# Operand tiles in a pool of their own, other holds of the shared PSUM bank, deferred squares and split key-value products in a one-layer hybrid trunk

## The chip, the cores and the metric

The kernel runs on one core of one Trainium2 chip. The metric is the device time of one execution in microseconds; the time before is 2718.81 us, the median of 3 runs (2717.66 to 2721.08). All times below are in microseconds (us) unless marked ns.

## What is computed

One layer of a hybrid encoder trunk on an input of 2048 positions by 1024 channels, in float32. Cut to what matters:

```
xn   = rmsnorm(h)
proj = xn @ w_in                       # columns split among three mixers
att  = chunked softmax attention       # 6 heads of 64, own chunk of 64 and 8 before it
conv = GLU, causal depthwise conv of 31 taps, LayerNorm, swish, pointwise projection
ret  = retention in chunks             # 6 heads of 64, rotary q and k, state carried along
h    = h + concat(att, conv, ret) @ w_o
h    = h + square(relu(rmsnorm(h) @ w1)) @ w2            # hidden size 4096
h    = h + sigmoid(rmsnorm(h) @ w_pg) * (p @ w_ple)
```

The retention's state needs, per head and chunk, the product of the decayed keys with the values (64 by 64).

## The kernel before

**Blocks and stages.** The sequence is worked in four blocks of T = 512 positions (four tiles of 128). A block goes through these stages, each a generator that issues matmuls and yields after each: conv_proj; the gate of the block before, in two halves; att_proj and ret_proj in turn for three pairs of heads (ap and rp); wo_a and wo_b (the output projection); ffn1 and ffn2 in eight groups, with ffn1 one group ahead; the gate of the last block comes at the end. Every large product is in split precision: an operand is a high part in fp32r and a low part, and `mm3s` (line 173) issues three matmuls of 512 columns, high with high, high with low, low with high. The output projection has 48 + 16 products of this kind per block, a group of ffn2 has 32, and the gate has 64 with the normalised residual and 16 with p.

**Tiles in SBUF.** There is a pool for constants, and then one pool, sp, for all else. A tag of a pool gets its place at its first use. In the compiled kernel, in bytes of a partition: constants from 1,152; w, the split weights, six buffers of 8,192 from 23,584; big slot 0 at 72,736 and slot 1 at 89,120 (16,384 each); the kv buffers (keys, queries, values, residual h) from 105,696; the work tiles behind them, with the convolution's yh and yl in 150,752 to 161,631 and the gate's p operand (ph, pl) in 172,640 to 180,831; big slot 2 at 195,712 and slot 3 at 212,096, up to 228,479. Slots 0 and 1 hold xh and xl, the high and low part of the normalised input, for conv_proj, the projections, ffn1, and the gate of the last block (`x3` in ffn2, line 739). Slots 2 and 3 hold in turn the mixers' output (mh, ml, line 458), the hidden layer (hid, two groups in turn, line 713) and xh, xl of the gate of the other blocks (`late`, line 753). In ap and rp the weights are the moving operand; everywhere else the weights are stationary and the tile of a big slot moves.

**The chains.** The mixers' own steps are three chains, generators that yield a delay after each step: att_mix (chain 0), ret_mix (chain 1), conv_mix (chain 2). `advance` (line 883), called after each yield of a stage, issues a chain's next step when the planner's clock `clk` (a sum of matmul costs in us, lines 46 to 59) has passed the step's delay. Chains 1 and 2 share one PSUM bank, `rbank` (line 112, one buffer), so they also wait for `rfree`, which is set 2.0 us ahead after each of their steps. When the position reaches a chain's end (lines 871 to 878), its steps are issued without either wait:

```
if t[1] > pos and clk[0] < (t[4] if c is chains[0] else max(t[4], rfree[0])):
    break
...
d = next(t[3])
t[4] = clk[0] + d + 0.01
if c is not chains[0]:
    rfree[0] = clk[0] + 2.0
```

The order of TensorE's instructions is kept as issued, so TensorE stands still when a step finds the bank not yet read out or its operand not yet made. The delays are in `W` (line 261): r0 3.5 after rkv, the key-value products; r1 2.4 after the transposes rqT and rkT; r2 1.8 after each score product rsc; c1 5.0 after cvt, the transposes before the convolution's LayerNorm, whose z is made on VectorE with a step on GpSimd (lines 395 to 403); c2 4.0 after cvb and cpw; qk 5.0, st 4.5 and ts 2.0 in attention.

**Squares.** `rms_split` (line 230) makes, for each of 8 channel tiles of h, the high part on ScalarE (L233), the low part on VectorE (L234), the square on ScalarE and, from the second tile on, the sum of squares on VectorE (L240). It is called in wo_b, in late and in the last ffn2. The sums go through a matmul with ones (ms) and come back as the row scale.

**Priorities.** All other orders are those of the scheduler, which goes by program order; `tc.high_priority(offset=n)` puts instructions n places forward, a negative n back (LATE is -1000).

Of the kernel before, what the change touches and what calls it, by code (L numbers as in the profile page):

```python
# [17 lines left out]
P = 128  # L18
D = 1024
S = 2048  # L20
T = 512
# [11 lines left out]
HALF = 512  # L33
AHEAD = 2500
LATE = -1000
AT, RT = (2, 4, 6), (3, 5, 7)
WOA = [(j, k) for ks in ((0, 1, 2, 3), (4, 5)) for j in range(2) for k in ks] + [(j, k) for j in range(2, KT) for k in range(6)]

# [2 lines left out]
def trunk(ctx, tc, a, out):  # L41
# [4 lines left out]
    class PE:  # L46
# [10 lines left out]
        def transpose(o, x, i):  # L57
            clk[0] += 240 / 2200.0
            tc.keep_in_program_order(nc.tensor.transpose(o, x, i))  # L59

    cpool = ctx.enter_context(tc.tile_pool(name="const", bufs=1))
    sp = ctx.enter_context(tc.tile_pool(name="sp", bufs=1))
    dram = ctx.enter_context(tc.tile_pool(name="dram", bufs=1, space=bass.MemoryType.DRAM))
# [9 lines left out]
    def stile(tag, bufs, shape, name=None, dt=F32):  # L73
        return sp.tile(list(shape), dt, tag=tag, name=name or tag, bufs=bufs)
# [2 lines left out]
        return stile("raw", 2, [P, UNIT], name)  # L77

    def big(name, slot):
        return stile(f"big{slot}", 1, [P, 8, T], name, F32R)  # L80

    def anat(name):
        return stile("anat", 5, [P, 256], name)
# [36 lines left out]


    def wtile():
        return stile("w", 6, [P, 2, 2, HALF], "w", F32R)

    def wsplit(w, x, n, eng):
        A.activation(w[:, 0, :n], x, AF.Copy)  # L126
# [103 lines left out]
    def rms_split(j, gidx, x, sq):  # L230
        h = cur["h"][j]
        g = ng[:, gidx, j : j + 1]
        A.activation(x[0][:, j], h, AF.Copy, scale=g)  # L233
        V.scalar_tensor_tensor(x[1][:, j], h, g, f(x[0][:, j]), ALU.mult, ALU.subtract)  # L234
        if j == 0:
            A.activation(sq, h, AF.Square)
        else:
            q = tmp("q", T)
            A.activation(q, h, AF.Square)
            V.tensor_tensor(sq, sq, q, ALU.add)  # L240

    def rms_rstd(r):
        b = rbank("ms")
# [139 lines left out]
    def conv_mix():  # L383
# [3 lines left out]
        for u in range(2):  # L387
            b = rbank("cvt")
            b2 = b.rearrange("p (t n) -> p t n", n=DC)
            s6 = stile("s6", 2, [P, 20])  # L390
            for i in range(2):
                t = 2 * u + i
                for c in range(2):
                    PE.transpose(b2[:, i, c * P : c * P + P], ys[c][:, t * P : t * P + P], ident)
            for i in range(2):
                V.bn_stats(s6[:, 6 * i : 6 * i + 6], b2[:, i])
                V.bn_aggr(s6[:, 12 + 2 * i : 14 + 2 * i], s6[:, 6 * i : 6 * i + 6])
            mv = s6[:, 12:16].rearrange("p (t c) -> p t c", c=2)
            V.tensor_scalar(s6[:, 16:18], mv[:, :, 1], EPS, None, ALU.add)
            rstd(s6[:, 18:20], s6[:, 16:18], 2)  # L400
            for i in range(2):
                V.tensor_scalar(z[u][:, i * DC : i * DC + DC], b2[:, i], s6[:, 12 + 2 * i : 13 + 2 * i],
                                s6[:, 18 + i : 19 + i], ALU.subtract, ALU.mult)
            yield W["c1"]
        hl = []
        for c in range(2):
            b = rbank("cvb")
            for t in range(NT):
                PE.transpose(b[:, t * P : t * P + P], z[t // 2][:, (t % 2) * DC + c * P : (t % 2) * DC + c * P + P], ident)
            u = tmp("u", T)  # L410
            A.activation(ys[c], b, AF.Tanh, bias=cvh[:, 1, c : c + 1], scale=cvh[:, 0, c : c + 1])
            A.activation(u, b, AF.Identity, bias=cvh[:, 1, c : c + 1], scale=cvh[:, 0, c : c + 1])
            V.scalar_tensor_tensor(ys[c], ys[c], 1.0, u, ALU.add, ALU.mult)
            yh, yl = cv("yh", F32R), cv("yl", F32R)
            A.activation(yh, ys[c], AF.Copy)
            V.tensor_tensor(yl, ys[c], f(yh), ALU.subtract)
            hl.append((yh, yl))
            yield W["c2"]
        yield W["c3"]
        for c in range(2):  # L420
            b = rbank("cpw")
# [178 lines left out]
    def ret_mix(p):  # L600
# [5 lines left out]
        st[p].reverse()  # L606
        b = rbank("rkv")
        for t in range(NT):
            PE.matmul(b[:, t * P : t * P + P], ns[t][:, P : 2 * P], ns[t][:, 256:384], start=True, stop=True)
        states = [now] + stm + [nxt]  # L610
        for t in range(NT):
            for hr in hrs:
                V.scalar_tensor_tensor(states[t + 1][hr, hr], states[t][hr, hr], gstate[hr, p : p + 1],
                                       b[hr, t * P + hr.start : t * P + hr.stop], ALU.mult, ALU.add)
        yield W["r0"]
        b = rbank("rqT")
        for t in range(NT):
            PE.transpose(b[:, t * P : t * P + P], ns[t][:, :P], ident)
# [1 line left out]
        for h, hr in enumerate(hrs):  # L620
            V.tensor_copy(qz[hr, :, h], b[hr].rearrange("p (t n) -> p t n", n=P))
        A.activation(qT, b, AF.Copy)
        yield W["r1"]
        b = rbank("rkT")
        for t in range(NT):
            PE.transpose(b[:, t * P : t * P + P], ns[t][:, P : 2 * P], ident)
        kT = stile("ro", 1, [P, T], "rk")
        A.activation(kT, b, AF.Copy)
        yield W["r1"]
        at = stile("rat", 1, [P, NT, 2 * P])  # L630
        mask = rm.rearrange("p h n -> p (h n)").unsqueeze(1).to_broadcast([P, 2, 2 * P])
        for u in range(2):
# [219 lines left out]

    chains = [[], [], []]
    rfree = [0.0]

    def chain(i, gen, start, end):
        chains[i].append([start, end, gen, None, 0.0])
# [24 lines left out]

    def advance(pos):
        posn[0] = pos
        for t in list(tasks):
            while t[0] and t[0][0] <= pos:
                t[0].pop(0)
                if t[2] is None:
                    t[2] = t[1]()
                next(t[2], None)  # L890
            if not t[0]:
                for _ in t[2]:
                    pass
                tasks.remove(t)
        for c in chains:
            while c and c[0][0] <= pos:
# [4 lines left out]
                    t[3] = t[2]()  # L901
                try:
                    d = next(t[3])
                    t[4] = clk[0] + d + 0.01
                    if c is not chains[0]:
                        rfree[0] = clk[0] + 2.0
                except StopIteration:
                    c.pop(0)

# [146 lines left out]
```

## Time and profile before

| | |
|---|---|
| median of 3 runs | 2718.81 us |
| lowest and highest | 2717.66 and 2721.08 us |
| profiled execution, device time | 2718.58 us |
| its span in the trace | 2716.6 us |
| TensorE busy | 2680.4 us, 99% |
| VectorE busy | 1327.8 us, 49% |
| ScalarE busy | 764.2 us, 28% |
| GpSimd busy | 97.0 us, 4% |
| DMA, share of 16 engines | 55.7%, mean 196 GB/s |

The profiled execution takes 2.0 us more than its span, what lies ahead of the first and behind the last instruction. Matmuls are pipelined: a group's mean is from the start to the end of one, and a new one starts before the last has ended, so the pace of a stream is read from the start of a run of matmuls to the start of the next.

### The profile page before, as it was taken

What the parts mean: (1) busy time and instruction counts of PE and PEld (TensorE: products, weight loads), DVE (VectorE), ACT (ScalarE), POOL (GpSimd) and SP (SyncE); (2) the same over time, 40 slices, a digit from 0 to 9 for tenths busy, and PEclk for the clock granted to TensorE, in tenths of its full rate; (3) what the DMA queues carried; (4) which work ended last, traced back from release to release, by engine and by line L of the source; (5) the groups of instructions that cost most, each with busy time, mean ns of one, the idle gap of its engine ahead of it and who ended that gap; (6) DMA issues with size and microseconds to landing.
All of it is one profiled execution on the core that took longest, in us unless ns stands there. A gap on an engine that the chain in (4) does not pass through costs nothing.

```text
span 2716.6 us, 33597 instructions
## 1 busy us (share of the span) xinstructions
PE 2680.4 (99%) x13354; PEld 2216.5 (82%) x13354; DVE 1327.8 (49%) x2649; ACT 764.2 (28%) x1576; POOL 97.0 (4%) x98
## 2 busy tenths in 40 slices
PE   8989999999999999999999999999999999999999
PEld 7777788888888888888888888888888888888887
DVE  7966544458655443334755552222384545222233
ACT  4444423343244222123214331101222432110111
POOL 1010000000010000000001000000000100000000
PEclk9999999999999999999999999999999999999999
DMA  8667656467633567677543455555654354555553
GB/s 285 211 213 244 219 177 208 166 198 267 217 121 140 206 216 261 216 255 261 217 168 121 159 203 192 193 186 191 240 194 170 112 199 142 189 191 187 192 201 125
DMA packets 123708, 533.36 MB, mean 196 GB/s; under 512 B 12832, under 2 KB 39712, under 8 KB 77728
## 3 DMA queue, kind: packets, MB, share of 16 engines
q1 hardware_dynamic: 123552, 531.21, 55.7%
q8 instruction: 106, 1.74, 0.3%
q14 instruction: 50, 0.41, 0.0%
HBM read 410.58 MB, written 120.59 MB: 196 GB/s over the span
## 4 chain that ended last, share of the span: by engine, by line
PE 89%; DVE 6%; DMA 2%; POOL 1%; ACT 1%; issue 1%; SPq 0%; POOLq 0%; DVEq 0%; ACTq 0%
PE acc L54 52%; PE w L54 27%; PE ple L54 2%; PE po L54 2%; PE sc L54 2%; PE sc L59 1%; POOL ass L199 1%; PE rout L54 1%; DVE y L359 1%; PE cvp L54 1%; DMA w<-k_wr 1%; DVE w L127 1%; PE rsc L54 1%; POOL g L199 0%; PE cpw L54 0%
## 5 line engine op out<-in xcount | busy, mean ns | idle before, releaser
L54 PE MATMUL acc<-xh,w 128*128 128x512 f32 (+1 forms) x1744 | 546.7, 389 | 0.0
L54 PE MATMUL acc<-w,xh 128*128 128x512 f32 (+1 forms) x1536 | 457.5, 373 | 1.1 <-DMA w<-k_wr 1.1
L54 PEld LDWEIGHTS acc<-xh,w 128*128 128x128 f32 x1744 | 326.3, 188 | 70.5 <-ACT xh L233 0.2
L54 PE MATMUL acc<-hid,w 128*128 128x512 f32 x1536 | 373.7, 396 | 0.0
L54 PE MATMUL w<-hid,w 128*128 128x512 f32 x1536 | 368.8, 395 | 0.0
L54 PEld LDWEIGHTS w<-hid,w 128*128 128x128 f32 x1536 | 288.5, 188 | 69.9
L54 PEld LDWEIGHTS acc<-hid,w 128*128 128x128 f32 x1536 | 288.7, 188 | 69.7
L54 PE MATMUL acc<-xl,w 128*128 128x512 f32 (+1 forms) x872 | 337.4, 391 | 1.9 <-DVE xl L234 1.9
L54 PE MATMUL w<-xh,w 128*128 128x512 f32 x1024 | 323.3, 391 | 0.0
L54 PEld LDWEIGHTS acc<-w,xh 128*128 128x128 f32 x1536 | 280.8, 189 | 38.9 <-issue 6.3
L126 ACT ACTIVATE w<-raw 128x512 fp32r<-128x512 f32 (+1 forms) x288 | 163.4, 615 | 460.6 <-PE acc L54 190.3
L54 PE MATMUL acc<-w,xl 128*128 128x384 f32 (+1 forms) x768 | 284.2, 370 | 0.0
L721 ACT ACTIVATE hid<-r 128x512 fp32r<-128x512 f32 x128 | 80.0, 625 | 569.3 <-DVE r L720 569.3
L54 PEld LDWEIGHTS w<-xh,w 128*128 128x128 f32 x1024 | 192.8, 189 | 39.7
L54 PE MATMUL w<-xl,w 128*128 128x512 f32 x512 | 200.1, 391 | 0.0
L54 PEld LDWEIGHTS acc<-xl,w 128*128 128x128 f32 x872 | 163.9, 188 | 38.3 <-DVE xl L234 4.2
L127 DVE TENSOR_TENSOR w<-raw,w 128x512 fp32r<-128x512 f32 (+1 forms) x288 | 182.7, 676 | 23.8 <-ACT w L126 23.1
L747 DVE TENSOR_TENSOR h<-h,w 128x512 f32<-128x512 f32 x128 | 88.0, 687 | 205.7 <-PE w L54 205.3
L359 DVE SCALAR_TENSOR_TENSOR y<-gl,cw,y 128x512 f32<-128x512 f32 x240 | 172.5, 745 | 1.9
L747 DVE TENSOR_TENSOR h<-h,acc 128x512 f32<-128x512 f32 x128 | 87.9, 687 | 169.9 <-PE acc L54 169.5
L54 PEld LDWEIGHTS acc<-w,xl 128*128 128x128 f32 x768 | 145.5, 189 | 15.7 <-issue 0.5
L720 DVE SCALAR_TENSOR_TENSOR r<-acc,r 128x512 f32<-128x512 f32 x64 | 44.3, 691 | 210.6 <-PE acc L54 197.7
(177 smaller groups left out, 2811.9 us busy)
## 6 DMA issues: line engine op xcount, KB each, us to landing
w<-k_w SPq DMA_DIRECT2D x160, 1024.0 KB, 4.8
k_w<-w SPq DMA_DIRECT2D x64, 1024.0 KB, 7.1
raw<-in_w_dram SPq DMA_DIRECT2D x96, 512.0 KB, 4.4
w<-k_wr SPq DMA_DIRECT2D x36, 1024.0 KB, 7.1
w<-k_w_g SPq DMA_DIRECT2D x30, 1024.0 KB, 4.8
w<-k_wa SPq DMA_DIRECT2D x36, 768.0 KB, 5.6
w<-k_w_oa SPq DMA_DIRECT2D x18, 1024.0 KB, 7.0
k_wr<-w SPq DMA_DIRECT2D x12, 1024.0 KB, 7.3
```

What stands on the lines that cost most here:

```text
L54: tc.keep_in_program_order(nc.tensor.matmul(o, x, y, start=start, stop=stop))
L59: tc.keep_in_program_order(nc.tensor.transpose(o, x, i))
L126: A.activation(w[:, 0, :n], x, AF.Copy)
L127: eng.tensor_tensor(w[:, 1, :n], x, f(w[:, 0, :n]), ALU.subtract)
L199: G.tensor_tensor(o, var, nhalf[:, :n], ALU.pow)
L359: V.scalar_tensor_tensor(y, gl[:, j : j + T], cw[:, c, j : j + 1], y, ALU.mult, ALU.add)
L720: V.scalar_tensor_tensor(r, b, 0.0, cur["r2"], ALU.max, ALU.mult)
L721: A.activation(hid[:, j], r, AF.Square)
L747: V.tensor_tensor(h[j], h[j], b, ALU.add)
```

## The change

There are four edits. The tags of the big slots and of w move out of sp into a pool gp that is opened before the constants. The squares of rms_split and their sum are put 150 places back. The planner's yields may give a second number, the time for which the shared bank is held (2.0 where none is given); cvt holds it for 5.0, cvb for 3.0, rkv for 3.5, rqT and rkT for 2.4; and both delays and holds are multiplied by 1.2 up to the start of the output projection of block 0. The key-value product of a tile, 128 by 128 with only the two diagonal blocks of 64 by 64 in use, is issued as the two diagonal blocks alone.

```diff
--- before.py
+++ after.py
@@ -33,6 +33,7 @@
 HALF = 512
 AHEAD = 2500
 LATE = -1000
+SQ = -150
 AT, RT = (2, 4, 6), (3, 5, 7)
 WOA = [(j, k) for ks in ((0, 1, 2, 3), (4, 5)) for j in range(2) for k in ks] + [(j, k) for j in range(2, KT) for k in range(6)]
 
@@ -58,6 +59,7 @@
             clk[0] += 240 / 2200.0
             tc.keep_in_program_order(nc.tensor.transpose(o, x, i))
 
+    gp = ctx.enter_context(tc.tile_pool(name="gp", bufs=1))
     cpool = ctx.enter_context(tc.tile_pool(name="const", bufs=1))
     sp = ctx.enter_context(tc.tile_pool(name="sp", bufs=1))
     dram = ctx.enter_context(tc.tile_pool(name="dram", bufs=1, space=bass.MemoryType.DRAM))
@@ -77,7 +79,7 @@
         return stile("raw", 2, [P, UNIT], name)
 
     def big(name, slot):
-        return stile(f"big{slot}", 1, [P, 8, T], name, F32R)
+        return gp.tile([P, 8, T], F32R, tag=f"big{slot}", name=name, bufs=1)
 
     def anat(name):
         return stile("anat", 5, [P, 256], name)
@@ -120,7 +122,7 @@
 
 
     def wtile():
-        return stile("w", 6, [P, 2, 2, HALF], "w", F32R)
+        return gp.tile([P, 2, 2, HALF], F32R, tag="w", name="w", bufs=6)
 
     def wsplit(w, x, n, eng):
         A.activation(w[:, 0, :n], x, AF.Copy)
@@ -232,12 +234,13 @@
         g = ng[:, gidx, j : j + 1]
         A.activation(x[0][:, j], h, AF.Copy, scale=g)
         V.scalar_tensor_tensor(x[1][:, j], h, g, f(x[0][:, j]), ALU.mult, ALU.subtract)
-        if j == 0:
-            A.activation(sq, h, AF.Square)
-        else:
-            q = tmp("q", T)
-            A.activation(q, h, AF.Square)
-            V.tensor_tensor(sq, sq, q, ALU.add)
+        with tc.high_priority(offset=SQ):
+            if j == 0:
+                A.activation(sq, h, AF.Square)
+            else:
+                q = tmp("q", T)
+                A.activation(q, h, AF.Square)
+                V.tensor_tensor(sq, sq, q, ALU.add)
 
     def rms_rstd(r):
         b = rbank("ms")
@@ -401,7 +404,7 @@
             for i in range(2):
                 V.tensor_scalar(z[u][:, i * DC : i * DC + DC], b2[:, i], s6[:, 12 + 2 * i : 13 + 2 * i],
                                 s6[:, 18 + i : 19 + i], ALU.subtract, ALU.mult)
-            yield W["c1"]
+            yield W["c1"], 5.0
         hl = []
         for c in range(2):
             b = rbank("cvb")
@@ -415,7 +418,7 @@
             A.activation(yh, ys[c], AF.Copy)
             V.tensor_tensor(yl, ys[c], f(yh), ALU.subtract)
             hl.append((yh, yl))
-            yield W["c2"]
+            yield W["c2"], 3.0
         yield W["c3"]
         for c in range(2):
             b = rbank("cpw")
@@ -606,13 +609,15 @@
         st[p].reverse()
         b = rbank("rkv")
         for t in range(NT):
-            PE.matmul(b[:, t * P : t * P + P], ns[t][:, P : 2 * P], ns[t][:, 256:384], start=True, stop=True)
+            for h, hr in enumerate(hrs):
+                PE.matmul(b[hr, t * P + h * HD : t * P + h * HD + HD], ns[t][:, P + h * HD : P + h * HD + HD],
+                          ns[t][:, 256 + h * HD : 256 + h * HD + HD], start=True, stop=True)
         states = [now] + stm + [nxt]
         for t in range(NT):
             for hr in hrs:
                 V.scalar_tensor_tensor(states[t + 1][hr, hr], states[t][hr, hr], gstate[hr, p : p + 1],
                                        b[hr, t * P + hr.start : t * P + hr.stop], ALU.mult, ALU.add)
-        yield W["r0"]
+        yield W["r0"], 3.5
         b = rbank("rqT")
         for t in range(NT):
             PE.transpose(b[:, t * P : t * P + P], ns[t][:, :P], ident)
@@ -620,13 +625,13 @@
         for h, hr in enumerate(hrs):
             V.tensor_copy(qz[hr, :, h], b[hr].rearrange("p (t n) -> p t n", n=P))
         A.activation(qT, b, AF.Copy)
-        yield W["r1"]
+        yield W["r1"], 2.4
         b = rbank("rkT")
         for t in range(NT):
             PE.transpose(b[:, t * P : t * P + P], ns[t][:, P : 2 * P], ident)
         kT = stile("ro", 1, [P, T], "rk")
         A.activation(kT, b, AF.Copy)
-        yield W["r1"]
+        yield W["r1"], 2.4
         at = stile("rat", 1, [P, NT, 2 * P])
         mask = rm.rearrange("p h n -> p (h n)").unsqueeze(1).to_broadcast([P, 2, 2 * P])
         for u in range(2):
@@ -852,6 +857,7 @@
 
     chains = [[], [], []]
     rfree = [0.0]
+    slow = [1.0]
 
     def chain(i, gen, start, end):
         chains[i].append([start, end, gen, None, 0.0])
@@ -882,6 +888,7 @@
 
     def advance(pos):
         posn[0] = pos
+        slow[0] = 1.2 if pos < at(("woa", 0), 0.0) else 1.0
         for t in list(tasks):
             while t[0] and t[0][0] <= pos:
                 t[0].pop(0)
@@ -901,9 +908,10 @@
                     t[3] = t[2]()
                 try:
                     d = next(t[3])
-                    t[4] = clk[0] + d + 0.01
+                    d, r = d if isinstance(d, tuple) else (d, 2.0)
+                    t[4] = clk[0] + d * slow[0] + 0.01
                     if c is not chains[0]:
-                        rfree[0] = clk[0] + 2.0
+                        rfree[0] = clk[0] + r * slow[0]
                 except StopIteration:
                     c.pop(0)
```

## Rows read from the trace of the kernel before

**Rows 1.** The page: the span, and busy time, share and instructions of TensorE.

```profile
span 2716.6 us, 33597 instructions
PE 2680.4 (99%) x13354; PEld 2216.5 (82%) x13354; DVE 1327.8 (49%) x2649; ACT 764.2 (28%) x1576; POOL 97.0 (4%) x98
```

**Rows 2.** Waits of TensorE: who, for whom, us in total, times, longest.

```profile
PE cvb L59 <- DVE z L402: 4.0, 3, 1.3
PE rsc L54 <- DVE rat L638: 3.6, 5, 1.1
PE rkv L54 <- DVE z L402: 3.0, 1, 3.0
PE sc L54 <- DVE pT L516: 2.4, 2, 2.2
PE rkT L59 <- ACT rq L622: 2.1, 2, 1.3
PE acc L54 <- DVE xl L234: 1.9, 3, 0.8
PE cvb L59 <- ACT rq L622: 1.9, 1, 1.9
PE sc L54 <- ACT k L202: 1.8, 1, 1.8
PE sc L54 <- DVE k L203: 1.5, 2, 1.0
```

**Rows 3.** Stretches of block 0: length, busy us by engine; third from last, granted clock.

```profile
69.00:76.00 7.00, 6.54 (x19) 5.20 (x20) 6.65 (x17) 1.27 (x6) 0.00 (x0) 0.51 0.74 268
158.00:161.30 3.30, 3.12 (x17) 2.72 (x17) 0.97 (x5) 0.00 (x0) 0.00 (x0) 0.50 0.06 25
171.60:175.00 3.40, 3.40 (x20) 2.63 (x19) 1.41 (x3) 2.32 (x4) 0.00 (x0) 0.51 0.00 0
284.20:287.60 3.40, 3.40 (x9) 2.65 (x8) 1.51 (x3) 1.15 (x2) 0.00 (x0) 0.50 0.09 28
```

**Rows 4.** Chain that ended last, feed-forward of block 0: start, us, what.

```profile
353.33 10.88 PE w L54 x48
...
372.46 5.60 PE w L54 x24
```

**Rows 5.** Groups of matmuls, shapes apart, whole span: count, busy us, mean ns, idle.

```profile
L54 PE MATMUL acc<-hid,w 128*128 128x512 f32 x1536 | 373.7, 396 | 0.0
L54 PE MATMUL w<-hid,w 128*128 128x512 f32 x1536 | 368.8, 395 | 0.0
L54 PE MATMUL w<-xh,w 128*128 128x512 f32 x1024 | 323.3, 391 | 0.0
...
L54 PE MATMUL ple<-pl,w 128*128 128x512 f32 x62 | 24.5, 395 | 0.0
...
L54 PE MATMUL cpw<-yh,pww 128*128 128x512 f32 x32 | 11.6, 405 | 0.0
```

**Rows 6.** Same view: output projection of block 1, gates of blocks 2 and 3.

```profile
926.17 17.73 PE acc L54 x76
...
2020.12 5.60 PE acc L54 x24
...
2677.82 5.49 PE acc L54 x24
```

**Rows 7.** Waits of TensorE in the mixers' stages of block 1 alone.

```profile
PE rsc L54 <- DVE rat L638: 0.5, 1, 0.5
```

**Rows 8.** VectorE in order of time at the start of block 0's feed-forward.

```profile
280.55 0.74 DVE L234 SCALAR_TENSOR_TENSOR xl<-h,ng,xh 128x512 fp32r<-128x512 f32 x1
281.21 0.68 DVE L240 TENSOR_TENSOR sq<-sq,q 128x512 f32<-128x512 f32 x1
```

**Rows 9.** Chain that ended last, mixers of block 1.

```profile
768.64 0.89 PE rkv L54 x8
...
772.48 1.24 PE po L54 x20
```

## The prediction

> **What bounds the kernel now.** I read the head of the page first. TensorE is busy for 2680.4 us of 2716.6 [rows 1], so only what TensorE does, or waits for, counts. VectorE, ScalarE and the queues matter where TensorE stands still for them. Three things can then be gained: waits of TensorE, stretches at the lower clock, and a shorter step from one matmul to the next.
>
> The list of waits, limited to TensorE, is short [rows 2]. The rows shown add up to 22.2 us. All but one belong to the chains (attention, retention, convolution), whose steps are strewn among the projections. The exception waits for the low parts of the normalised residual at the start of the feed-forward stage (L234). The 3.0 us before rkv are one wait on z (L402): the retention chain asked for the shared bank while the convolution chain's statistics still read it.
>
> The table by stretches shows what such waits cost on top [rows 3]. In four stretches of block 0, 17.1 us together, the granted clock is 0.50 or 0.51, the 1.2 GHz level; the timeline puts waits of [rows 2] right before each: rkv's 3.0 us before 158, cvb's 1.9 on rq before 171.6, the scores' 1.8 and then 1.0 on k before 69, the three on xl, 1.9 in all, before 284.2. At half the clock, half of a busy stretch is lost: 3.5, 1.6, 1.7 and 1.7 us.
>
> The chain of work that ended last gives the step of the large matmuls. In the first feed-forward product 48 matmuls take 10.88 us, 226.7 ns each; in the second, 24 take 5.60 us, 233.3 ns each [rows 4]. Both have 512 moving columns and three matmuls per product. The averages over the whole trace say the same, 391 ns against 395 and 396 [rows 5]. What differs is the moving operand: slots 0 and 1 (bytes 72,736 to 105,503) in the first, hid in slots 2 and 3 (195,712 to 228,479) in the second. The gate is the better test, being the same code twice: for blocks 0 to 2 it reads slots 2 and 3, and 24 matmuls take 5.60 us; for block 3 it reads slots 0 and 1, and 24 take 5.49 us [rows 6]. The output projection, which reads slots 2 and 3, is at 17.73/76 = 233.3 ns. So the rate goes with the place of the moving operand.
>
> **The change part by part,** against the profiled execution: 2718.58 us, of which 2.0 lie around the span; it stands 0.2 under the median of 2718.81, so I take both as one.
>
> **A, the pool.** The new pool comes first, so w fills bytes 1,152 to 50,303 and slots 0 to 3 fill 50,304 to 115,839 (six times 8,192, four times 16,384). No moving operand of a projection lies high any more. hid: 2 x 1536 matmuls [rows 5] x 6.6 ns = 20.3 us. Output projection: 4 blocks x 64 products x 3 = 768 matmuls x 6.6 = 5.1. Gate of three blocks: 24 groups x 0.11 = 2.6 [rows 6]. Together 28.0. What lay between slots 1 and 2 moves up by 32,768 bytes. The gate's p operand lay high before and already takes 395 ns [rows 5], so it loses nothing. The keys under the scores (504 matmuls, two at a time) move from 105,696 to 138,464 and on; no row shows them there, so they cost between nothing and 252 x 6.6 ns = 1.7 us, and I take 1.0, above the middle, since every high operand in the rows is slow. Net -27.0. The bounds are -28 and -15: slot 3 ends in 99,456 to 115,839, and nothing in the rows reads beyond 105,503 fast, so half of the gain could stay away. Here a rule speaks against the change.
>
> The Trainium skill, "TensorE: Matmul & The Clock Gate", section "Back-to-back issue gap", gives a warm matmul of 512 columns 216 ns wherever its operand lies, and "SBUF — State Buffer", section "Who interferes with whom", says that TensorE never waits on anyone there; by these A would be 0 and the sum 2700. The trace has 226.7 and 233.3 ns and disagrees; the rows decide.
>
> **B, the chains.** In block 0 every own delay becomes 1.2 times as long, and a step that leaves long work behind keeps the bank reserved for longer (planner microseconds, which I take as real ones). rkv after cvt: 2.0 becomes 6.0, so the wait of 3.0 and its slow clock of 1.6 go: -4.6. cvb after rqT: 2.0 becomes 2.9: -0.9 of 1.9, and half of the 1.7, since the wait stays half as long. First scores, 1.8 + 1.0 behind k: the delay grows by 1.0, so -1.0; their 3.5 us of clock I count at -1.0, between 0 and -3.5, because nearly two thirds of the wait stay. Scores behind pT, 2.2: -0.9. rkT, two waits of 2.1 together, delay +0.5: -1.0. rsc, two of about 1.1, delay +0.4: -0.7. Together -11.0. In blocks 1 to 3 only the holds change. rsc loses 0.5 each [rows 7] because cvt slips in ahead of it; a hold of 5.0 instead of 2.0 sends rsc later: -1.5. The 1.3 us before cvb stay, for c1 was 5.0 already and z is late behind retention's VectorE work. B is -12.5. The bounds are -20 and +3: no row shows these chains with longer holds, and a later step can meet another wait. Behind a step held back waits only the rest of its own chain; the projections go on meanwhile. A chain that gets so late that it reaches its deadline issues without any delay; that is in the upper bound.
>
> **C, squares.** VectorE alternates xl (0.74 us) and sq (0.68) one for one [rows 8], while TensorE wants an xl per matmul. With the squares behind, xl comes every 0.6 us or so rather than every 1.26, and block 0 loses its 1.9 us and the slow clock, 1.7: -3.5. Blocks 1 to 3 have no such row and gain nothing. What could be late next is the mean-square matmul that reads sq; VectorE's work before it is the same in sum, so it is done by about the same moment, but TensorE gets there some 3.5 us earlier. Bounds -4 to +1.
>
> **D, key-value products.** Eight instructions in 0.89 us become sixteen with half the stationary and half the moving columns. The nearest row is po: 64 stationary columns, two halves side by side, 20 in 1.24 us, 62 ns each [rows 9], but 128 moving columns. Sixteen at 62 are 0.99, and 0.50 if half the columns halve it: per product +0.10 to -0.39, over 12 products +1.2 to -4.7. I take -2.0, near the middle.
>
> Sum: -27.0 - 12.5 - 3.5 - 2.0 = -45.0, so 2718.6 - 44.7 = **2674 us**. With every term at its good end it is 2662 (-28 -20 -4 -4.7), with every term at its bad end 2709 (-15 +3 +1 +1.2), for which four things have to go wrong at once.
>
> **The rivals.**
> 1. The place of the operand is not the cause, A is 0. For it: nothing in the page names a port or an address. Against it: the gate at two rates with the same code [rows 6]. Time: 2718.6 - 18.0 = 2700. (The two pages above would have it so.) Chance 0.10.
> 2. The longer holds give nothing: the waits in block 0 move to other steps, since VectorE has the same work to do, and the clock falls as before. For it: most of these waits are on VectorE, which the holds don't relieve [rows 2]. Against it: the longest, rkv's, is an order of steps that the holds forbid. Time: 2718.6 - 27.0 - 3.5 - 2.0 = 2686. Chance 0.18.
> 3. Slower: it is the start of the operand, not its height, that sets the rate. xh starts 32 bytes past a multiple of 64 (72,736) and is fast; hid starts on a multiple of 128 (195,712) and is slow. The new pool starts at 1,152, nine times 128, and all its tiles would be slow. Then A is no gain, and conv, first feed-forward product and last gate, 384 + 3072 + 192 matmuls, pay 6.6 ns (24 us), and the projections that move w pay 1152 x 6.6 + 1152 x 5.0 (13 us): 2718.6 + 37 - 18.0 = 2738. It decides once some 2,700 of these matmuls slow down (18.0 / 6.6 ns). Against it: pl and yh (172,640 and on, and 150,752 and on, all 32 past a multiple of 64) take 395 and 405 ns, not the 391 of xh [rows 5]. Chance 0.04.
> 4. The parts cancel within the noise. Chance 0.03.
>
> **How the numbers follow.** The forecast has what is left, 0.65. Two runs of this kernel differ by up to 0.13%, so 0.2%, or 5.4 us, is what a measurement can tell from no change. Faster: 0.65 + 0.18 + 0.10 = 0.93; same 0.03; slower 0.04. The range takes in the forecast with its bounds and rival 2, and half of rival 1: 2660 to 2700.
>
> **What would show it.** A: the chain has 24 matmuls of the second feed-forward product in about 5.45 us instead of 5.60, and 5.49 in the gate of every block. If hid still takes 396 ns on average, A is wrong; if xh rises to 396, it is rival 3. B: no wait of rkv on z, and a granted clock of 1.00 in the stretch that answers to 158; sc behind k still waits. If the waits of TensorE in block 0 add up to over 15 us, rival 2. C: no wait on L234, and no new one before ms. D: a rkv group under 0.89 us. Wrong altogether it would be if the span stayed over 2705.

## The result, and the profile after

The changed kernel takes 2681.54 us, the median of 4 runs (2681.03 to 2685.79), beside 2718.23 us for the kernel before (4 runs, 2716.89 to 2721.08): a ratio of 0.9867, with a 95% interval of 0.9850 to 0.9884. By the ratio that is 36.2 us less (gains of runs below are also given by their ratio, taken on 2718 us). It lies within the range given, 7.5 us over the forecast of 2674. The profiled execution took 2681.23 us. Two single executions, 8963.00 us of e1_pool below (its profiled one) and 5370.15 us of the kernel before, are left out of all figures. The head of its page answers to [rows 1]: the span is 37.2 us shorter, and TensorE is busy for 34.3 us less.

```profile
span 2679.4 us, 33782 instructions
PE 2646.1 (99%) x13450; PEld 2209.8 (82%) x13450; DVE 1328.7 (50%) x2649; ACT 765.3 (29%) x1576; POOL 96.5 (4%) x98
```

**The pace of the matmuls.** The chain that ended last, of the changed kernel (start, us, what), answers to [rows 4], [rows 6] and [rows 9]:

```profile
344.47 10.88 PE w L55 x48
...
363.51 5.44 PE w L55 x24
...
754.52 0.62 PE rkv L55 x16
...
915.79 12.52 PE acc L55 x55
...
1990.05 5.46 PE acc L55 x24
1995.51 1.40 PE ple L55 x6
```

The first feed-forward product keeps its 226.7 ns (10.88/48). The second has come down to the same pace: 24 matmuls in 5.44 us instead of 5.60. The gate of block 2 takes 5.46 instead of 5.60, and the output projection 227.6 ns a matmul (12.52/55) instead of 233.3. A key-value group (rkv) takes 0.62 us instead of 0.89. Only the matmuls of the gate's p operand (ple) are at 233.3 ns (1.40/6); in the kernel before they were a little faster, at 230 (1.38/6, shown with the table below). The groups by form, which answer to [rows 5], say the same (count, busy us, mean ns):

```profile
L55 PE MATMUL acc<-hid,w 128*128 128x512 f32 x1536 | 363.1, 389 | 0.0
L55 PE MATMUL w<-hid,w 128*128 128x512 f32 x1536 | 358.6, 389 | 0.0
L55 PE MATMUL w<-xh,w 128*128 128x512 f32 x1024 | 323.1, 391 | 0.0
...
L55 PE MATMUL ple<-pl,w 128*128 128x512 f32 x62 | 24.6, 396 | 0.0
```

**The waits.** TensorE's waits in the changed kernel (who, for whom, us, times, longest) answer to [rows 2]:

```profile
PE cvt L60 <- DVE z L405: 5.8, 3, 1.9
PE cvt L60 <- DVE y L362: 3.6, 1, 3.6
PE sc L55 <- DVE pT L519: 2.3, 2, 2.0
PE ms L55 <- DVE sq L243: 1.9, 2, 1.7
PE cpw L55 <- DVE ml L431: 1.6, 1, 1.6
...
PE sc L55 <- DVE k L205: 1.0, 1, 1.0
PE sc L55 <- ACT k L204: 0.9, 1, 0.9
PE rkT L60 <- ACT rq L627: 0.9, 2, 0.5
...
PE cvb L60 <- DVE z L405: 0.7, 1, 0.7
```

The rkv wait of 3.0 us is gone, as are those of rsc (3.6), of cvb on rq (1.9) and of the residual's low part (1.9). In their place stand four that the kernel before did not have: cvt on z, cvt on y, ms on sq, cpw on ml. With the lines left out, and without the opening waits of cvp, the list adds up to 21.0 us; the same list of before adds up to 23.8 ([rows 2] and 1.6 us in two small lines). So 2.8 us of waiting went away, while the names on it changed almost wholly.

**The clock.** Four stretches of 3.4 us are at the 1.2 GHz level (length, busy us by engine, granted clock third from last); the fifth line is the stretch that answers to the one after rkv's wait in [rows 3], now at the full clock:

```profile
92.60:96.00 3.40, 3.40 (x14) 2.87 (x15) 2.27 (x7) 1.31 (x4) 0.00 (x0) 0.52 0.92 386
147.20:150.60 3.40, 3.40 (x13) 3.40 (x12) 2.52 (x8) 0.00 (x0) 0.70 (x1) 0.52 1.07 429
280.40:283.80 3.40, 3.40 (x10) 2.69 (x10) 0.16 (x1) 0.00 (x0) 1.01 (x1) 0.53 0.84 343
2116.70:2120.10 3.40, 3.40 (x11) 2.82 (x11) 1.75 (x7) 0.00 (x0) 0.70 (x1) 0.52 0.02 5
...
151.00:170.00 19.00, 18.51 (x129) 15.80 (x128) 11.27 (x32) 9.43 (x24) 3.03 (x3) 1.00 0.31 112
```

That is 13.6 us at half the clock instead of 17.1. Half of such a stretch is lost, so the clock gives back 1.75 us. Each begins no more than 1.4 us behind the end of a wait in the list above: the scores' on pT (92.48 us), cvt's on y (145.82), ms's on sq (279.33) and, in block 3, cvt's on z (2116.50). The last three are new.

**Where the new waits come from.** The timeline of the changed kernel shows the three kinds (start, us, engine, what, and in brackets the idle time before and its releaser):

```profile
141.95 0.27 PE L60 MATMUL cvt<-ident,y 128*128 128x128 f32 x1
145.02 0.74 DVE L362 SCALAR_TENSOR_TENSOR y<-gl,cw,y 128x512 f32<-128x512 f32 x1
145.82 0.55 PE L60 MATMUL cvt<-ident,y 128*128 128x128 f32 x3 [3.60 <-DVE y L362]
...
279.33 1.08 PE L55 MATMUL ms<-ones,sq 128*128 128x1 f32 x8 [1.67 <-DVE sq L243]
...
2109.00 0.60 PE L60 MATMUL cvt<-ident,y 128*128 128x128 f32 x4
...
2115.45 0.99 DVE L405 TENSOR_SCALAR z<-cvt,s 128x256 f32<-128x256 f32 x2 [0.68 <-POOL s L201]
2116.50 1.11 PE L60 MATMUL cvt<-ident,y 128*128 128x128 f32 x4 [1.95 <-DVE z L405]
```

In block 0 the first cvt is issued at 141.95, where the kernel before had it at 146.17, and VectorE ends the last of the convolution's taps at 145.76 (145.02 + 0.74), where it ended it at 143.91 before. TensorE comes earlier and VectorE later, and the difference is the wait of 3.6. In blocks 1 to 3 the second cvt comes 7.5 us after the first and meets the bank that z is still being read from. In the kernel before, retention's steps lay between the two (in block 3 at 2127.85 and 2144.14), and the wait was at the next step, cvb. The price hardly differs: in block 1 alone the waits of the mixers are 1.9 us now, against 2.0 before, which was 1.3 at cvb, the 0.5 of [rows 7] and 0.2 at rqT.

### The profile page after: what moved, and what is told of

Its sections match the earlier page's. It is cut to its first block, busy times and chain, and to the rows that moved or that the text cites. A ratio compares the mean times of both kernels' runs of the same rounds, so it can differ in the third digit from the quotient of the medians.

```text
span 2679.4 us, 33782 instructions
## 1 busy us (share of the span) xinstructions
PE 2646.1 (99%) x13450; PEld 2209.8 (82%) x13450; DVE 1328.7 (50%) x2649; ACT 765.3 (29%) x1576; POOL 96.5 (4%) x98
## 3 DMA queue, kind: packets, MB, share of 16 engines
q8 instruction: 107, 1.75, 0.3%
## 4 chain that ended last, share of the span: by engine, by line
PE 91%; DVE 4%; DMA 2%; POOL 1%; ACT 1%; issue 0%; SPq 0%; DVEq 0%; POOLq 0%; ACTq 0%
PE acc L55 53%; PE w L55 27%; PE sc L60 2%; PE sc L55 2%; PE po L55 2%; PE ple L55 2%; PE rout L55 1%; DVE w L129 1%; DVE y L362 1%; PE cvp L55 1%; PE rsc L55 1%; DMA w<-k_wr 1%; POOL g L201 0%; DMA raw<-in_w_oa_dram 0%; PE cpw L55 0%
## 5 line engine op out<-in xcount | busy, mean ns | idle before, releaser
L55 PE MATMUL acc<-hid,w 128*128 128x512 f32 x1536 | 363.1, 389 | 0.0
L55 PE MATMUL w<-hid,w 128*128 128x512 f32 x1536 | 358.6, 389 | 0.0
L55 PEld LDWEIGHTS acc<-w,xl 128*128 128x128 f32 x768 | 145.3, 189 | 17.1 <-issue 1.5
```

The lines of the kernel that those rows point to most:

```text
L55: tc.keep_in_program_order(nc.tensor.matmul(o, x, y, start=start, stop=stop))
```

## The experiments

Spans below are those of the profiled executions, and 2716.6 is that of the kernel before [rows 1]. Runs of one kernel differ by 1 to 6 us.

### Each part alone

**e1_pool**: the kernel before with the pool alone.

```diff
+    gp = ctx.enter_context(tc.tile_pool(name="gp", bufs=1))
     cpool = ctx.enter_context(tc.tile_pool(name="const", bufs=1))
...
-        return stile(f"big{slot}", 1, [P, 8, T], name, F32R)
+        return gp.tile([P, 8, T], F32R, tag=f"big{slot}", name=name, bufs=1)
...
-        return stile("w", 6, [P, 2, 2, HALF], "w", F32R)
+        return gp.tile([P, 2, 2, HALF], F32R, tag="w", name="w", bufs=6)
```

> The kernel before with the new pool alone. Place theory: 24 matmuls of the second feed-forward product in about 5.45 us instead of 5.60, the mean of hid's matmuls near 389 ns instead of 396, the mixers' waits as before; 2718 - 27 = 2691 us, between 2687 and 2695. Rival (the place is no cause, the gain of the full change comes from elsewhere): no change, 2718.

Measured: 2692.18 us, ratio 0.9895 (0.9878 to 0.9911), or 28.5 us less. The pool is worth what was forecast. Rows for this edit are read from e7_shift32 below, which differs from it by 32 bytes.

**e2_chains**: the kernel before with the holds, and the factor of 1.2, alone.

```diff
-            yield W["c1"]
+            yield W["c1"], 5.0
...
-        yield W["r0"]
+        yield W["r0"], 3.5
...
+        slow[0] = 1.2 if pos < at(("woa", 0), 0.0) else 1.0
...
+                    t[4] = clk[0] + d * slow[0] + 0.01
...
+                        rfree[0] = clk[0] + r * slow[0]
```

> The kernel before with the delays and holds of the chains alone. Theory from the changed kernel's trace (the waits are exchanged, not removed): the wait of rkv on z goes, waits of cvt on z (some 1.9 us per block) and of cvt on the last taps (about 3 us in block 0) come; mixers' stages of blocks 1 to 3 the same within 0.5 us each, block 0 shorter by 4 to 7 us; 2711 to 2715 us. Rival (the holds are worth what was forecast): 2706 us. Second rival (exchange in full): 2718.

Measured: 2711.47 us, ratio 0.9969 (0.9956 to 0.9982), or 8.4 us less; the span is 6.8 us shorter. From TensorE's waits of this kernel:

```profile
PE cvt L59 <- DVE z L402: 5.8, 3, 1.9
...
PE cpw L54 <- DVE ml L428: 1.6, 1, 1.6
...
PE rkv L54 <- DVE z L402: 0.3, 1, 0.3
```

rkv's wait falls from 3.0 to 0.3, and cvt on z and cpw on ml appear here already: these two come with this part (e8_holds below parts the holds from the factor). The list is 19.9 us long against 23.8. So part B gives two thirds of its 12.5 us when it stands alone, since some of the waits went to other steps.

**e3_squares**: the kernel before with the squares put back alone.

```diff
+        with tc.high_priority(offset=SQ):
+            if j == 0:
+                A.activation(sq, h, AF.Square)
...
```

> The kernel before with the squares behind alone. Theory: the three waits on xl in block 0 (1.9 us) go, the mean-square matmul waits for sq instead, 1.5 to 2.5 us, and the slow clock that follows comes a little later all the same; the first group of the feed-forward of block 0 shortens by under 1 us, the total is within 1.5 us of 2718. Rival (the forecast): that group 3.5 us shorter, 2714.5 us, no wait before ms.

Measured: 2715.56 us, ratio 0.9987 (0.9977 to 0.9996), or 3.5 us less (1.1 to 6.3 by the interval); the span of the one execution is 1.5 us shorter. The new wait before ms is the one expected; the total is 2.4 us under 2718, where within 1.5 us was expected. The wait on xl is gone from its list of TensorE's waits, and this line has come:

```profile
PE ms L55 <- DVE sq L242: 1.7, 1, 1.7
```

The wait went from the first matmuls of the stage, 1.9 us, to the mean-square matmul, 1.7 us, and the stretch at half the clock, which was at 284.2 us, is now at 288.2. The runs show a small gain, but the trace shows no wait removed; where the gain comes from was not settled.

**e4_halves**: the kernel before with the key-value products in halves alone.

```diff
-            PE.matmul(b[:, t * P : t * P + P], ns[t][:, P : 2 * P], ns[t][:, 256:384], start=True, stop=True)
+            for h, hr in enumerate(hrs):
+                PE.matmul(b[hr, t * P + h * HD : t * P + h * HD + HD], ns[t][:, P + h * HD : P + h * HD + HD],
+                          ns[t][:, 256 + h * HD : 256 + h * HD + HD], start=True, stop=True)
```

> The kernel before with the key-value products in halves alone. If two halves run side by side: a group of sixteen instructions in 0.50 to 0.60 us instead of 0.89, 12 groups, -3.5 to -4.7 us, 2714 us. If they run as po does whatever the moving columns: 0.99 us, +1.2 us, 2719. Forecast: between, about 0.72 us, -2 us.

Measured: 2715.37 us, ratio 0.9985 (0.9976 to 0.9994), or 4.1 us less; the span is 4.8 us shorter. Its chain of work that ended last has

```profile
766.68 0.62 PE rkv L54 x16
```

Sixteen instructions take 0.62 us, 39 ns each, where eight of the full size took 0.89 [rows 9]: 12 x 0.27 = 3.2 us. In the list of TensorE's waits this line is new:

```profile
PE cvt L59 <- DVE y L359: 3.1, 1, 3.1
```

So the wait of cvt on the last taps is no doing of the holds: it comes when the first cvt is issued earlier, at 142.52 us here. Other waits became shorter in exchange, that of the scores on pT from 2.4 to 1.0 and that of rkv from 3.0 to 2.2.

The four alone add up to 44.5 us by their ratios, and to 41.5 by the profiled spans (28.4 for the pool, from e7_shift32, 6.8, 1.5, 4.8). Together they gave 36.2 and 37.2. Each interval is some 2.5 to 4.5 us to either side, so the size of the shortfall, 4 to 8 us, is not sure; the exchange of waits above is where the trace shows it.

### Why the pool is worth 28 us

The prediction said height in the partition. Three kernels with the pool alone at other places, and three with the tiles at other distances from each other, test that. The traces show no addresses: all bytes below are worked out from the layouts given above.

**e5_high**: the pool is opened after sp, so that w starts at 114,048, slots 0 and 1 at 163,200 and 179,584, slots 2 and 3 at 195,968 and 212,352: every operand lies high.

```diff
     sp = ctx.enter_context(tc.tile_pool(name="sp", bufs=1))
+    gp = ctx.enter_context(tc.tile_pool(name="gp", bufs=1))
```

> The kernel before with the same new pool, but opened after the others, so that w begins at byte 114,048, xh at 163,200, xl at 179,584, the other two slots at 195,968 and 212,352. Place theory (a moving operand high in the partition costs some 6.6 ns a matmul): hid stays at 5.60 us for 24, the first feed-forward product goes to the same pace (48 in 11.2 us instead of 10.88), 3648 matmuls, +24 us; where w moves, 0 to +13 us more: 2742 to 2755. Rival (a pool of its own helps, wherever it lies): 2691. Rival (the place is no cause): 2718.

Measured: 2689.02 us, ratio 0.9893 (0.9879 to 0.9908). Its group of the second feed-forward product:

```profile
L54 PE MATMUL w<-hid,w 128*128 128x512 f32 x1536 | 358.5, 389 | 0.0
```

hid lies 256 bytes above its place in the kernel before, and is fast. Height is not the cause.

**e6_middle**: the kv buffers in a pool of their own ahead, then the pool; w starts at 50,208, slot 2 at 132,128.

```diff
+    kvp = ctx.enter_context(tc.tile_pool(name="kvp", bufs=1))
+    gp = ctx.enter_context(tc.tile_pool(name="gp", bufs=1))
...
-        return stile("kv", 17, shape, name, dt)
+        return kvp.tile(list(shape), dt, tag="kv", name=name, bufs=17)
```

> The kernel before with w at byte 50,208, xh at 99,360, xl at 115,744, the other two slots at 132,128 and 148,512. If the pace changes at one height between 115,840 and 132,128: xh and xl fast but for the end of xl, hid slow in both slots as before, 24 in 5.60 us; total 2716 to 2722. If the height is between 164,896 and 195,712: everything fast, 2691. If the price grows with the height: hid between, about 24 in 5.52 us, 2705.

Measured: 2689.90 us, ratio 0.9898 (0.9883 to 0.9912), the same mean:

```profile
L54 PE MATMUL w<-hid,w 128*128 128x512 f32 x1536 | 358.6, 389 | 0.0
```

**e7_shift32**: e1_pool with 32 unused bytes ahead of all tiles of the pool.

```diff
+    gp.tile([P, 8], F32, tag="pad", name="pad", bufs=1)
```

> The kernel before with the new pool alone, as in e1_pool, all its tiles 32 bytes further on (starts 32 past a multiple of 128, as xh had before). Place theory: the same as e1_pool, 2691 us, 24 matmuls on hid in 5.45 us, and a page by which the pool alone can be read. Rival (the alignment of the start has a part in the gain): another pace than 226.7 ns, 2700 or more.

Measured: 2689.69 us, ratio 0.9896 (0.9881 to 0.9911); its span is 2688.2, 28.4 less than before.

```profile
L54 PE MATMUL w<-hid,w 128*128 128x512 f32 x1536 | 358.6, 389 | 0.0
```

The start of all tiles together does not matter either, so the third rival falls in the form it was given. What the fast kernels share is the distance between w and the slots.

**e9_pad32**: the kernel before, with 32 unused bytes ahead of slot 2, so that slots 2 and 3 lie 32 bytes higher.

```diff
+            if "pad" not in cur:
+                cur["pad"] = stile("pad", 1, [P, 8])
             cur["m"] = big("mh", 2), big("ml", 3)
```

> The kernel before, one pool as it was, with an unused tile of 32 bytes ahead of big slot 2: slots 2 and 3 move from byte 195,712 to 195,744 and now start at 32 past a multiple of 128, as w and slots 0 and 1 do. New theory (the pace depends on whether the moving operand and the weights start at the same remainder to 128; it is slow where they differ): hid 24 in 5.45 us, output projection and the gates fast, 2690 us, the whole gain of the pool. Rival (w and the four slots must be in one pool, or side by side): no change, 2718. The forecast's theory (height): no change, 2718.

Measured: 2716.73 us, ratio 0.9994 (0.9984 to 1.0004), no difference:

```profile
L54 PE MATMUL w<-hid,w 128*128 128x512 f32 x1536 | 368.8, 395 | 0.0
```

The distance from w to slot 2 is now 172,160 bytes, a multiple of 128, and the pace is the slow one; a multiple of 128 is not enough.

**e10_offset64**: e1_pool with 64 unused bytes between w and the slots.

```diff
+    gp.tile([P, 16], F32, tag="pad", name="pad", bufs=1)
```

> The new pool alone, as in e1_pool, with an unused tile of 64 bytes between w and the four slots: everything low, side by side and in one pool, but every projection now has operands whose starts differ by 64 in their remainder to 128. New theory: all projections slow, first and second feed-forward product alike, 226.7 becoming 229 to 234 ns; 2710 to 2755 us. If the remainder to 64 is what counts: fast, 2690. Rivals (height, one pool, side by side): fast, 2690.

Measured: 2709.22 us, ratio 0.9966 (0.9954 to 0.9978): two thirds of the pool's gain are gone. Its groups, and then its chain:

```profile
L54 PE MATMUL w<-hid,w 128*128 128x512 f32 x1536 | 362.0, 391 | 0.0
L54 PE MATMUL w<-xh,w 128*128 128x512 f32 x1024 | 325.0, 393 | 0.0
```

```profile
351.64 10.99 PE w L54 x48
...
370.87 5.49 PE w L54 x24
```

Both feed-forward products now go at 229 ns (10.99/48, 5.49/24), the one slower than before and the other faster. One pool, low in the partition and side by side, is not enough.

**e12_pads**: the kernel before with its one pool, and unused bytes ahead of slot 2 (160) and slot 3 (256).

```diff
+                cur["pad"] = stile("pad", 1, [P, 40])
+            mh = big("mh", 2)
...
+                cur["pad3"] = stile("pad3", 1, [P, 64])
+            cur["m"] = mh, big("ml", 3)
```

> The kernel before, one pool, with an unused tile of 160 bytes ahead of slot 2 and one of 256 ahead of slot 3: slot 2 starts at 195,872, a multiple of 256 but not of 512 away from w (23,584), slot 3 at 212,512, a multiple of 512 away. Theory (the pace is fast where moving operand and weights start a multiple of 512 bytes apart, and neither pool nor height counts): hid of the odd groups (slot 3) 24 in 5.45 us, of the even groups (slot 2) in 5.60, about 2705 us. If a multiple of 256 is enough: both fast, 2690 us. Rivals (one pool or side by side is needed; height): both slow, 2718.

Measured: 2690.77 us, ratio 0.9902 (0.9885 to 0.9918):

```profile
L54 PE MATMUL acc<-hid,w 128*128 128x512 f32 x1536 | 363.1, 389 | 0.0
L54 PE MATMUL w<-hid,w 128*128 128x512 f32 x1536 | 358.5, 389 | 0.0
```

416 bytes of padding do what the pool does. (By the table below the first 160 would be enough, since slot 3 would then lie 737 times 256 bytes from w; that was not tried.) By the distance from the start of w, and what remains of it after whole multiples of 256 bytes, the measured paces fall into one order (the last column is the step from one matmul to the next in the chain that ended last):

| kernel | moving tile | distance from w, bytes | remainder by 256 | mean ns | step, ns |
|---|---|---|---|---|---|
| before | xh, slot 0 | 49,152 | 0 | 391 | 226.7 |
| e5, e6, e7, after | hid, slot 2 | 81,920 | 0 | 389 | 226.7 |
| e12 | hid, slots 2 and 3 | 172,288; 188,928 | 0 | 389 | 226.7 |
| e10 | hid, slot 2 | 81,984 | 64 | 391 | 229 |
| before | p operand, ph; pl | 149,056 | 64 | 392; 395 | 230 |
| before | hid, slot 2 | 172,128 | 96 | 395 | 233.3 |
| e9 | hid, slot 2 | 172,160 | 128 | 395 | 233.3 |
| e10 | p operand, ph; pl | 204,320 | 32 | 395; 392 | 233.3 |
| after | p operand, ph; pl | 204,256 | 224 | 396; 396 | 233.3 |

The p operand's rows are these, the first of the kernel before and the second of e10_offset64:

```profile
2025.72 1.38 PE ple L54 x6
```

```profile
2010.60 1.40 PE ple L54 x6
```

The means alone do not give this order: that of pl is 395 at 64 and 392 at 32. Within the tiles the operands step by 512 and by 2,048 bytes, so the remainder is the same for every matmul of a stream. Remainders of 160 and 192 were not met in these streams, those of 32 and 224 only by the p operand; in the projections of the mixers w is the moving operand, and no row here shows their step alone. Why the chip does this no run shows.

### Versions that go further

**e8_holds**: the changed kernel without the factor of 1.2.

```diff
-        slow[0] = 1.2 if pos < at(("woa", 0), 0.0) else 1.0
+        slow[0] = 1.0 if pos < at(("woa", 0), 0.0) else 1.0
```

> The changed kernel without the factor 1.2, with the longer holds. If the factor carries what block 0 gained: its waits on k, rq and rat come back, some 4 us with a slow stretch, 2685 to 2688. If the holds carry it: 2681, the same as the changed kernel. If the factor only moved TensorE into later waits (cvt on the taps): 2679 or less.

Measured: 2678.95 us (2677.31 to 2679.55), ratio 0.9855 (0.9839 to 0.9872). That is 2.6 us under the changed kernel by the medians, with intervals that overlap. From its list of TensorE's waits:

```profile
PE cvt L60 <- DVE z L405: 6.0, 3, 2.1
PE cvt L60 <- DVE y L362: 3.4, 1, 3.4
...
PE sc L55 <- ACT k L204: 1.8, 1, 1.8
```

The wait of cpw on ml is gone, so it came from the factor, and that of the first scores is back at 1.8; rkv does not wait here either. So it is the holds that removed rkv's wait, and the longer delays are worth nothing here, or less.

**e11_best**: the changed kernel without the factor, with what the waits and the table ask for: the convolution's chain in block 0 starts later, c1 and its hold are 7.5, the second normalisation of block 0 starts its work a little later, and the buffers that hold the gate's p operand (and other tiles) move into the pool, to a multiple of 256 bytes from w.

```diff
-        return stile("rnat", 4, [P, 512], name)
+        return gp.tile([P, 512], F32, tag="rnat", name=name, bufs=4)
...
-            yield W["c1"], 5.0
+            yield W["c1"] + 2.5, 7.5
...
-            chain(2, conv_mix, at(("ap", b, 2), 0.1), at(("rp", b, 2), 0.9))
+            chain(2, conv_mix, at(("ap", b, 2), 0.35), at(("rp", b, 2), 0.95))
...
-        place(norm2, [at(("g1", b, 0), NE), at(("g1", b, 0), NF)])
+        place(norm2, [at(("g1", b, 0), NE + (0 if b else 0.12)), at(("g1", b, 0), NF + (0 if b else 0.12))])
```

> The changed kernel without the factor 1.2; the buffers of the gate's p operand in the new pool too, so that they start at the same remainder as w; cvt's delay and hold at 7.5; the convolution chain of block 0 a quarter of a projection later, its end from 0.90 to 0.95; the mean square of block 0 somewhat later. Theory: ple's matmuls at 389 ns instead of 396 (-1.3 us), no wait of cvt on z (-6.0), none on the taps (-3.4 and the slow clock behind it), none of ms on sq in block 0 (-1.7 and the slow clock); 2663 to 2669 us. Rival (each wait is only exchanged for another): 2677 to 2680.

Measured: 2665.55 us (2663.36 to 2666.44), ratio 0.9805 (0.9787 to 0.9822): 16.0 us under the changed kernel, the fastest of all. Its span, three of its waits, and the gate's p operand in its chain:

```profile
span 2663.4 us, 33785 instructions
```

```profile
PE sc L55 <- DVE pT L519: 4.0, 4, 1.7
...
PE cpw L55 <- DVE ml L431: 1.6, 1, 1.6
...
PE ms L55 <- DVE sq L243: 0.5, 1, 0.5
```

```profile
2004.41 1.36 PE ple L55 x6
```

No cvt waits any more, while the scores on pT wait longer than in the changed kernel (4.0, 2.3) and cpw waits 1.6 as there; the whole list, again without cvp, is 11.9 us instead of 21.0. The stretches at half the clock go from 13.6 us to one of 3.4, near 198 us, which gives back 5.1 us. The p operand goes at 226.7 ns a matmul (1.36/6), 1.3 us less over its two largest groups (44.1 + 24.6 against 43.2 + 24.2). That makes 15.5 of the 16.0 us. The edits were not run one by one.

## Why the prediction was right, and where not

**A, the pool: forecast -27.0, measured -28.4** (the span of e7_shift32). The terms hold: the second feed-forward product 3072 x 6.7 ns = 20.5 us (20.3 forecast), the output projection 768 x 5.7 ns = 4.4 (5.1), the gate 24 x 0.14 = 3.4 (2.6). The keys under the scores, which I priced at 1.0 us, cost nothing: their 512-column group has a mean of 418 ns, and 419 before. The p operand, which I had at no loss, goes from 230 to 233.3 ns, some 0.6 us over its 186 matmuls. But the step "so the rate goes with the place of the moving operand" was wrong as I used it, for height. Two slow places and one fast place told only that place matters; I took the one property, height, that fitted, and used the pl and yh rows as proof of it. The rows fit a remainder of the distance from w as well: 96 for hid, 64 for pl, 0 for xh. The chain could have warned me: there the p operand, high as it lies, goes at 230 ns and not at hid's 233.3, which its mean of 395 hides. That the size came out right is luck of a kind: the new pool has w and all four slots next to each other, so all distances are multiples of 256. Had the pool held 64 more bytes between them, as e10_offset64 has, some 19 of the 28 us would have stayed away (28.5 less 9.2). The third rival was nearest in kind, since it asked for the start of the tile, but it looked at the start alone; e7_shift32 answers that. The first rival, that place does not count, falls.

The Trainium skill, "SBUF — State Buffer", section "Who interferes with whom", gives TensorE two read ports, one for the moving operand and one for the weight load, and calls them independent. In time the two are not independent here: the same moving tile, hid, goes at 226.7, 229 or 233.3 ns by its distance from the weights. Through what, no run shows.

**B, the chains: forecast -12.5, and C, squares: forecast -3.5; together they gave about -5.5 here** (-37.2 less 28.4 for A and 3.2 for D, rounded). The waits and the clock of the two traces account for most: 2.8 + 1.75 = 4.6 us. The waits that B names did fall, and by more than forecast. Without the one on xl, [rows 2] has 20.3 us of them; 6.2 are left (cvb on z, the scores, rkT, and 0.4 on rat at rout), 14.1 less, where the sum has 9.0 beside its 3.5 for the clock. rkv's wait went, the first scores' on k fell from 3.3 to 1.9 and rkT's from 2.1 to 0.9, about as priced; the scores' on pT stayed.

What failed is that the sum has no term for a wait at another step. To put a wait of w behind a delay that grows by d down as w less d holds the moment at which the operand is made fixed, and holds all other steps in place. Neither stays, and 11.8 us of new waits came: 5.8 at cvt on z, 3.6 at cvt on y, 1.6 at cpw, 0.8 on rn. In block 0 the first cvt came 4.2 us earlier and its operand 1.9 us later. By e4_halves this wait comes with D, and a slow stretch follows it at 147.20 as one followed rkv's before, so the clock that rkv's wait gave back was lost again 11 us earlier. In blocks 1 to 3 retention's steps no longer lay between the two cvt, and "a hold of 5.0 instead of 2.0 sends rsc later: -1.5" came true for rsc, whose waits went, while cvt took up 1.9 us a block. cpw got its 1.6 us with the factor: the second cpw comes 3.2 us behind the first (205.05 and 201.85), the wait included, where it was 5.5 before. That is less than its delay, and fits a chain that has reached its deadline, a case that I had named, though only for the bound. The second rival, that the waits move, was right for most of B, since 11.8 of the 14.1 us came back at other steps, and its time of 2686 is nearer to the 2681.5 measured than the forecast of 2674: I gave it too small a chance.

In C the sentence on the bound was the right one: the sum of squares is done no earlier, TensorE gets there earlier, and ms waits 1.7 us for it. In its own runs the part still gained 3.5 us, so its size is open between these two readings.

My mark for rival 2, over 15 us of waits in block 0, was badly placed. The kernel after has 13.9 us there, the one before 16.8: under the mark, and yet most of the expected gain was missing. The sum says less than the list.

**D, key-value halves: forecast -2.0, measured 12 x 0.27 = -3.2.** I took the middle between 0.50 and 0.99 us a group; it is 0.62, since halves of 64 columns side by side cost 39 ns an instruction where po, with 128 moving columns, has 62 [rows 9]. The end of the range that scaled with the columns was the nearer one. The Trainium skill, "TensorEngine Tiling (Array Packing)", section "Key Properties", says that different tiles of the array can load weights and multiply in parallel; the trace agrees, with 16 instructions in 0.62 us where 8 whole ones took 0.89: in the group at 754.5 us the two halves of a pair start 6 or 7 ns apart, and from the second pair on the next pair 58 or 59 ns after.

So of the sum, -45.0 against -37.2, A was 1.4 and D 1.2 us better than forecast, and B with C some 10.5 worse. (The 44.7 in the prediction's last subtraction is a slip for 45.0; both give 2674.)

## What to carry to other kernels

Where the same matmul goes at two rates, compare the addresses of both its operands, and test with a pad of a few hundred bytes before naming a cause: here 416 unused bytes were worth 1%. A longer delay shrinks the wait that it stands before, but an engine that has the same work to do is met by another step; ask when each operand is then made, and which step comes first, and give the sum a term for the wait there. Here a longer hold of a shared buffer paid where the order of two chains was at fault, and a general factor on all delays did not.

## What the runs showed of the hardware that was not expected

The pace of a stream of 512-column fp32r matmuls, each with its own weights, depends on the distance in bytes between the moving operand and the weights: 226.7 ns where it is a multiple of 256, 229 to 230 ns at a remainder of 64, 233.3 ns at 96 and 128, and for the p operand at 32 and 224. The place of both together, from 1,152 to 114,048 for w, changes nothing that the means show (389 ns).

Short waits cost more than their length: the waits of 1.7, 1.9, 2.0 and 3.6 us in the changed kernel were each followed, within 1.4 us, by 3.4 us at a granted clock of 0.52 or 0.53. Not each such wait is: the same 1.9 us before cvt in blocks 1 and 2 was not, for the stretches from 700 to 800 us and from 1200 to 1800, which hold them, have a granted clock of 1.00.
